# The last modulation block shared out anew between VectorE and TensorE, and the folded h fetched on GpSimd's queue

## The chip, the cores and the metric

The kernel runs on one core of a Trainium2 chip. A core has TensorE (matrix products; PE in the profile, PEld for its weight loads), VectorE (DVE), ScalarE (ACT), GpSimd (POOL) and SyncE (SP), which issues most of the DMAs. The metric is the device time of one launch, in microseconds (us); the time of before is the median of three runs.

## The reference

One layer of a diffusion backbone, in float32, for 128 context and 256 latent positions at width 2048. The part that the change touches is the adaptive modulation: for two condition vectors (context, latent), `silu(cond) @ w_ada + b_ada` gives six vectors of 2048 per condition, which shift, scale and gate the two sub-layers.

```python
mod = jax.nn.silu(cond) @ lw['w_ada'] + lw['b_ada']
sh1, sc1, ga1, sh2, sc2, ga2 = [m[:, None, :] for m in jnp.split(mod, N_MOD, axis=-1)]
h = rmsnorm(x, lw['norm_pre_mix']) * (1.0 + sc1) + sh1
m, s_f, s_b = mixer(h, s0_f, s0_b, n_chunks, lw)   # GLA and Fourier branches, gates, w_out
x = x + ga1 * rmsnorm(m, lw['norm_post_mix'])
h = rmsnorm(x, lw['norm_pre_ffn']) * (1.0 + sc2) + sh2
ff = (jax.nn.silu(h @ lw['w_ffn_gate']) * (h @ lw['w_ffn_up'])) @ lw['w_ffn_down']
x = x + ga2 * rmsnorm(ff, lw['norm_post_ffn'])
```

## The kernel before

Activations stand transposed (128 channels on the partitions, 384 positions along the free side). A weight half of 128x1024 comes by DMA (`raw`), ScalarE rounds it (`whi`, L256), VectorE takes the rest (`wlo`, L257), and TensorE makes three products per 128 columns (`A_hi,whi`, `A_lo,whi`, `A_hi,wlo`, L291). Weights are prepared some halves ahead, in four pairs of buffers. TensorE, ScalarE, VectorE and GpSimd each run their instructions in the order in which the program is written; nothing is reordered.

The stages follow each other: first norm and first modulation with the V projection; Q and K with the gated linear attention (GLA) beside the gate projections; gate units 22 and 23 with the folding of h for the Fourier branch; units 24 to 31 with the Fourier products; the merge; the output projection `w_out` (16 units of two halves of 24 products); a short stage that normalises and makes the input of the FFN; the FFN.

Side work is written as Python generators that are stepped once for each half (24 products):

- `ada_rest` (L656): modulation blocks (m, half) for m = 2, 3, 4. Each block takes 16 granules of `w_ada` (128x1024, tile `adaw`, two buffers); for a granule VectorE runs two operations, one for each condition, into `adacc` (L664 for the first granule, L666 for the others). Then eight small products sum over the partitions (L676), ScalarE copies (L640), two transposes (L644) and four small VectorE operations (L649 to L654) finish it. Five of the six blocks are made so.
- `ada_pe` (L684): the sixth block, (4, 1), is made by TensorE alone, four groups of four granules (tile `adax`), 16 products a group (L701), six steps apart, in the `w_out` stage. It ends in `ada_finish` (tile `evp`).
- `rate` (L715) says how many operations of `ada_rest` a step takes: in the GLA stage the number that the GLA generator yields, then 2.25 beside the Fourier products and 1.35 in `w_out`. After unit 12 of `w_out` both generators are run to their end.
- `folding` fetches the folded h (`hf_d`) in four pieces of 768 KB into two buffers (`fx`, L987 on SyncE's queue); `parts_of` (L1003) runs four products on each and splits it (L331, L332). The weights `wn` of these products are cleared by GpSimd (L994) and written by VectorE (L996). Ahead of that GpSimd clears `nyq` (L979), once the GLA stage's last ScalarE work on `qk` is done.

The stage ahead of the FFN (L1338 to L1470) sums squares (`wide_sum`), makes row factors `prow` (`rows2`, L1348), and fills two gaps with idle products on ones (`narrow_warm`, L1357). Then a loop over k makes h for channel tile k: VectorE `z` (L1412, L1418), ScalarE scale and shift with `mods` and rounding (`A_hi`, L1420, L1424), VectorE `A_lo` (L1436), VectorE and GpSimd the new x ahead of it (`t`, L1380; L1384), and TensorE the products of tile k-1 for three units of the FFN at once (L1454).

Of the kernel before, what the change touches and what calls it, by code (L numbers as in the profile page):

```python
# [11 lines left out]
F32 = mybir.dt.float32  # L12
# [9 lines left out]
P = 128  # L22
D = 2048
KT = D // P
TC = 128
TL = 256
T = TC + TL
# [10 lines left out]
G = 1024  # L38
# [69 lines left out]
def tile_step(ctx: ExitStack, tc: tile.TileContext, a, o):  # L108
    nc = tc.nc
    PE, ACT, DVE, POOL, SP = nc.tensor, nc.scalar, nc.vector, nc.gpsimd, nc.sync  # L110
# [80 lines left out]
    HEAD = 3  # L191
# [169 lines left out]
    hf_d = dram.tile([P, KT, T], F32, name="hf_d")  # L361
# [277 lines left out]
    def ada_finish(m, half, pr, ev):  # L639
        ACT.copy(ev, pr)  # L640
        yield True
        pt = pss.tile([P, 2, P], F32, tag="side", name="ptm")
        for b in range(2):
            PE.transpose(pt[:, b, :], ev[:, b * P : (b + 1) * P], ident)  # L644

        src = pt.rearrange("p b (j r) -> p j b r", r=32)
        mh = mods[:, m, 8 * half : 8 * half + 8, :]
        for c in range(2):
            DVE.tensor_copy(mh[:, :, c].rearrange("p (j b) -> p j b", b=2), src[:, :, :, c])  # L649
# [6 lines left out]
    def ada_rest(blocks):  # L656
        for m, half in blocks:
            acc = adap.tile([P, 2, 1024], F32, tag="adacc", name="adacc")
            for k in range(KT):
                w = adap.tile([P, 1024], F32, tag="adaw", name="adaw", bufs=2)  # L660
                SP.dma_start(w, a["w_ada"][m - 2, half, k])
                for c in range(2):
                    if k == 0:
                        DVE.tensor_scalar_mul(acc[:, c, :], w, cond[:, k, c : c + 1])  # L664
                    else:
                        DVE.scalar_tensor_tensor(  # L666
                            acc[:, c, :], w, cond[:, k, c : c + 1], acc[:, c, :], op0=ALU.mult, op1=ALU.add,
                        )
# [5 lines left out]
            for c in range(2):  # L674
                for j in range(4):
                    PE.matmul(  # L676
                        pr[32 * j : 32 * j + 32, :], selr[:, 32 * c : 32 * c + 32],
                        acc[:, c, j * 256 : (j + 1) * 256], start=c == 0, stop=c == 1,
                    )
            yield from ada_finish(m, half, pr, acc[:, 0, 0:256])  # L680

    def ada_pe(pool, cpad, ev, m, half, apart):

        def fetch(k0):  # L684

            ws = []
            for n, t in enumerate(("hid_hi", "hid_lo", "S0", "S1")):
                ws.append(pool.tile([P, G], F32, tag=t, name="adax", bufs=1))
                SP.dma_start(ws[n], a["w_ada"][m - 2, half, k0 + n])
            return ws  # L690

        pr = None
        for k0 in range(0, KT, 4):
            ws = fetch(k0)
            for _ in range(apart):
                yield
            if pr is None:
                pr = pss.tile([P, 256], F32, tag="side", name="pr")
            for n, w in enumerate(ws):
                for j in range(4):  # L700
                    PE.matmul(  # L701
                        pr[32 * j : 32 * j + 32, :], cpad[:, k0 + n, :], w[:, j * 256 : (j + 1) * 256],
                        start=k0 + n == 0, stop=k0 + n == KT - 1,
                    )
        yield from ada_finish(m, half, pr, ev)


    gates_d = dram.tile([32, P, T], F32, name="gates_d")
# [4 lines left out]
        return qk[:, h:8:4, t * P : (t + 1) * P]  # L713

    rate = [1.0]  # L715
    ada_gen = ada_rest([(m, half) for m in (2, 3, 4) for half in range(2)][:-1])
# [13 lines left out]
    with ExitStack() as s:  # L730
# [28 lines left out]
        def gla():  # L759
# [10 lines left out]
            for h in range(NH):  # L770
# [201 lines left out]
    with ExitStack() as s:  # L972
# [11 lines left out]
        fx = actp.tile([P, 2, 4, T], F32, tag="C_lo", name="fx")  # L984

        def fetch(b):
            SP.dma_start(fx[:, b % 2], hf_d[:, 4 * b : 4 * b + 4, :])  # L987

        fetch(0)
        fetch(1)  # L990
# [251 lines left out]
    with ExitStack() as s:  # L1242
# [16 lines left out]
        by_pe = ada_pe(pe, cpad, pd.tile([P, 256], F32, name="evp", bufs=1), 4, 1, 6)  # L1259

        qs = [pd.tile([P, T], F32, tag=f"qs{n}", name="qs", bufs=1) for n in range(3)]

# [78 lines left out]

        r = pd.tile([P, 2, 3], F32, name="r12", bufs=1)
        u = pd.tile([P, 2, 3], F32, name="u12", bufs=1)
        prow, prow2 = (pss.tile([P, T], F32, tag="side", name="prow") for _ in range(2))

        def rows2(dst, n):
            for t in range(3):
# [4 lines left out]
        hp = [psm.tile([P, T], F32, tag="mm", name="pmm") for _ in range(HEAD - 1)]  # L1352

        def narrow_warm(n):

            for _ in range(n):
                PE.matmul(hp[-2][:, 0:P], ones, ones, start=True, stop=True)  # L1357
# [81 lines left out]
        for k in range(KT + 1):  # L1439
            if k < KT:  # L1440
                res_b(k)
            if k:
                res_c(k - 1)

            for n in range(k + 2 + (k > 4), k + 3 + (k > 3)):
                if n < KT:
                    res_m(n)
                    res_a(n)
            if k:
                if k % 8 == 1:  # L1450
                    hw = [take() for _ in range(HEAD)]
                for j, m in ((0, 0), (1, 0), (0, 1)):
                    for u in range(HEAD):
                        PE.matmul(  # L1454
                            hp[u], hw[u][j][:, ((k - 1) % 8) * P : ((k - 1) % 8 + 1) * P], h2[m][:, k - 1, :],
                            start=k == 1 and j == m == 0, stop=k == KT and m == 1,
                        )
            if k in (9, 12):
                split(None, POOL)
                load()  # L1460
# [262 lines left out]
        n = 0  # L1723
# [500 lines left out]
```

## Time and profile before

| | us |
|---|---|
| median of three runs | 1922.1 (1920.74 to 1923.08) |
| the profiled execution | 1921.57 |
| its span | 1919.8 |
| granted TensorE clock in it | 0.998 of full speed |

The stages stand in the span (us) at 146 to 418 (Q, K, GLA), 418 to 437 (folding), 437 to 612 (Fourier products), 612 to 741 (merge), 741 to 877 (`w_out`), 877 to 911 (ahead of the FFN); the rest is the FFN. A row of the timeline gives the start, the duration, the engine, the line and operation, out<-in with shapes, how many, and in brackets the idle time of the engine just before and what ended it. A TensorE product of float32 operands counts as two records in the trace, so 16 products of L701 stand as x32. Products overlap in the pipeline: the distance from one start to the next is what a product costs, not its duration.

### The profile page before, as it was taken

Reading aid. Unit: us, or ns where it says so; the run is one execution under the profiler, and the core shown is the slowest. Engines: PE = TensorE matmul, PEld = TensorE weight load, DVE = VectorE, ACT = ScalarE, POOL = GpSimd, SP = SyncE. Lnnn points to the kernel's source line nnn. Section 1 sums busy time; section 2 is a strip of 40 time slices with the busy share of each in tenths; the row PEclk is TensorE's granted clock in tenths of the full one; section 3 lists DMA queues with packets and bytes.
Section 4 is the critical chain, followed back from the end, with each engine's and each line's share of the span. In section 5 each row is a group of like instructions: output and inputs, shape, how many; then the busy total and the mean of one; then the engine's idle time right before and its main releaser. Section 6 shows DMA issues by size and latency. Waiting matters only on the chain.

```text
span 1919.8 us, 28034 instructions
## 1 busy us (share of the span) xinstructions
PE 1898.7 (99%) x10396; PEld 1674.6 (87%) x10396; DVE 1634.2 (85%) x2104; ACT 1080.2 (56%) x1569; POOL 160.4 (8%) x189
## 2 busy tenths in 40 slices
PE   8999999999999999999999999999999999999997
PEld 5779999999999999999988888888888888888886
DVE  5677878787977897877799999999999999988985
ACT  4335545554447554446457666756666666666554
POOL 0000001000000000004000111111112021111001
PEclk9999999999999999999999999999999999999999
DMA  9986767777756787765449697988879797969563
GB/s 389 371 316 217 230 219 229 242 255 240 245 189 195 254 278 266 277 227 203 160 135 282 158 253 179 249 198 229 206 216 234 185 247 179 264 128 260 147 209 114
DMA packets 247529, 435.66 MB, mean 227 GB/s; under 512 B 45916, under 2 KB 150556, under 8 KB 242784
## 3 DMA queue, kind: packets, MB, share of 16 engines
q1 hardware_dynamic: 199792, 391.59, 61.1%
q0 software_dynamic: 18944, 33.63, 11.4%
q10 hardware_dynamic: 28656, 8.65, 2.5%
q8 instruction: 81, 1.33, 0.3%
q14 instruction: 56, 0.46, 0.1%
HBM read 369.05 MB, written 57.67 MB: 222 GB/s over the span
## 4 chain that ended last, share of the span: by engine, by line
PE 88%; DVE 4%; DMA 4%; ACT 2%; issue 1%; SPq 0%; DVEq 0%; ACTq 0%
PE pgu L1740 31%; PE pmm L291 26%; PE pdn L1740 10%; PE pds L1740 7%; PE pv L463 3%; PE pgm L446 1%; PE pfo L1103 1%; DVE wlo L257 1%; DMA slab<-in_w_ada 1%; PE px L481 1%; PE pmm L1454 1%; DMA raw<-in_w_gate 1%; ACT whi L256 1%; DMA raw<-in_w_out 1%; PE pfo L1104 1%
## 5 line engine op out<-in xcount | busy, mean ns | idle before, releaser
L291 PE MATMUL pmm<-A_hi,whi 128*128 128x384 f32 x1072 | 361.7, 337 | 0.0
L291 PE MATMUL pmm<-A_lo,whi 128*128 128x384 f32 x1072 | 358.6, 335 | 0.5 <-DVE A_lo L332 0.5
L291 PE MATMUL pmm<-A_hi,wlo 128*128 128x384 f32 x1072 | 358.7, 335 | 0.0
L1638 ACT CAST whi<-u 128x1024 fp32r<-128x1024 f32 x200 | 210.3, 1053 | 171.2 <-PE pds L1740 40.8
L1649 DVE TENSOR_TENSOR wlo<-u,whi 128x1024 fp32r<-128x1024 f32 x200 | 243.6, 1220 | 34.6 <-ACT whi L1638 32.5
L256 ACT CAST whi<-raw 128x1024 fp32r<-128x1024 f32 x163 | 170.7, 1051 | 158.5 <-DMA raw<-in_w_out 66.9
L1740 PE MATMUL pgu<-whi,A_hi 128*128 128x512 f32 x640 | 249.9, 391 | 0.0
L1740 PE MATMUL pgu<-whi,A_lo 128*128 128x512 f32 x640 | 249.1, 389 | 0.0
L257 DVE TENSOR_TENSOR wlo<-raw,whi 128x1024 fp32r<-128x1024 f32 x161 | 196.0, 1219 | 52.4 <-ACT whi L256 51.7
L1638 ACT CAST whi<-raw 128x1024 fp32r<-128x1024 f32 x157 | 164.9, 1052 | 91.3 <-PE pgu L1740 30.0
L291 PEld LDWEIGHTS pmm<-A_hi,whi 128*128 128x128 f32 x1072 | 201.2, 188 | 4.7 <-issue 3.3
L1649 DVE TENSOR_TENSOR wlo<-raw,whi 128x1024 fp32r<-128x1024 f32 x157 | 191.1, 1217 | 13.3 <-ACT whi L1638 11.3
L291 PEld LDWEIGHTS pmm<-A_lo,whi 128*128 128x128 f32 x1072 | 201.3, 188 | 1.0 <-DVE A_lo L332 0.8
L291 PEld LDWEIGHTS pmm<-A_hi,wlo 128*128 128x128 f32 x1072 | 201.2, 188 | 0.0
L666 DVE SCALAR_TENSOR_TENSOR adacc<-adaw,cond,adacc 128x1024 f32<-128x1024 f32 x150 | 187.6, 1278 | 12.9 <-DMA adaw<-in_w_ada 12.4
L1740 PE MATMUL pgu<-wlo,A_hi 128*128 128x512 f32 x640 | 185.7, 389 | 0.0
L1740 PEld LDWEIGHTS pgu<-whi,A_hi 128*128 128x128 f32 x640 | 120.1, 188 | 25.9 <-issue 0.8
L1740 PEld LDWEIGHTS pgu<-wlo,A_hi 128*128 128x128 f32 x640 | 120.2, 188 | 25.1
L1740 PEld LDWEIGHTS pgu<-whi,A_lo 128*128 128x128 f32 x640 | 120.2, 188 | 24.7
L1740 PE MATMUL pgu<-whi,S 128*128 128x512 f32 x400 | 116.6, 389 | 0.0
L1873 POOL DMA_DIRECT2D sums_d<-spare x64 | 58.3, 952 | 623.6 <-ACT spare L1869 602.3
L1740 PE MATMUL pdn<-whi,hid_hi 128*128 128x512 f32 x264 | 102.8, 389 | 0.0
(465 smaller groups left out, 3538.4 us busy)
## 6 DMA issues: line engine op xcount, KB each, us to landing
adaw<-in_w_ada SPq DMA_DIRECT2D x80, 512.0 KB, 4.4
raw<-in_w_d SPq DMA_DIRECT2D x70, 512.0 KB, 5.9
slab<-in_w_ada SPq DMA_DIRECT2D x32, 1024.0 KB, 9.5
raw<-in_w_gate SPq DMA_DIRECT2D x64, 512.0 KB, 4.6
raw<-in_w_g SPq DMA_DIRECT2D x48, 512.0 KB, 3.7
raw<-in_w_u SPq DMA_DIRECT2D x48, 512.0 KB, 5.1
u<-in_w_u SPq DMA_DIRECT2D x40, 512.0 KB, 6.0
u<-in_w_g SPq DMA_DIRECT2D x40, 512.0 KB, 9.3
```

The source lines that it names most:

```text
L256: ACT.copy(hi, raw)
L257: sub = lambda: eng.tensor_sub(lo, raw, hi.bitcast(F32))
L291: PE.matmul(dst, w[wi][:, k * n + n0 : k * n + n0 + P], x[xi][:, k0 + k, :], start=first and k == 0 and j == 0, stop=last and k == kts - 1 ...
L446: PE.matmul(pgv[q : q + 32, :], spad[:, k, :], slab[k // (KT // 2)][:, k % (KT // 2), :], start=k < 4, stop=k >= KT - 4,)
L463: PE.matmul(pv[2 * t + g], hT[x_][:, kb, t * P : (t + 1) * P], w_[:, g * 512 : (g + 1) * 512], start=kb == 0 and j == 0, stop=kb == KT - 1 ...
L481: PE.matmul(px, w_[:, u * P : (u + 1) * P], hT[x_][:, kb, :], start=j == 0, stop=j == 2)
L666: DVE.scalar_tensor_tensor(acc[:, c, :], w, cond[:, k, c : c + 1], acc[:, c, :], op0=ALU.mult, op1=ALU.add,)
L1103: PE.matmul(p, w[0][:, c], x[:, 0 : 2 * n], start=kh == k == 0, stop=False)
L1638: ACT.copy(hi, src)
L1649: DVE.tensor_sub(lo, src, hi.bitcast(F32))
L1740: PE.matmul(dst, stat[x_][m], mov(w[w_], m), start=first and w_ == m == x_ == 0, stop=last and w_ == m == 1, skip_group_check=any(more),)
L1873: POOL.dma_start(sums_d[k], u, accum_op=ALU.add)
```

## The change

Three things are changed.

1. The blocks. `ada_rest` takes the sixth block too, for its first 9 granules. `ada_pe` is left with one group of four granules (9 to 12), whose products go into the same accumulator as the partition sums of VectorE's part (`ada_products`, `ada_sums`), and are copied to `evp0`. The last three granules are loaded as halves into `ep0` to `ep5`, and their products (`late_products`) take the place of `narrow_warm(4)` and `narrow_warm(2)`; their sums stand in spare columns 384 to 511 of the PSUM banks of `prow` and of two of the three FFN accumulators. At k = 3 and k = 4 ScalarE copies these to `evp1` and `evp2`; at k = 6 six float32 products with the identity transpose the three parts and add them up, and `ada_finish`, now only four VectorE operations, writes `mods` for tiles 8 to 15. Granules of `adax` are fetched one a step instead of four at once.
2. The folded h is fetched by GpSimd's queue.
3. The GLA generator yields 3 or 4 where it yielded 2, for another of its steps less; `rate` becomes 2.5 beside the Fourier products and 1.75 in `w_out`.

```diff
+    def ada_sums(pr, acc, first, last):
+        for c in range(2):
+            for j in range(4):
+                PE.matmul(
+                    pr[32 * j : 32 * j + 32, :], selr[:, 32 * c : 32 * c + 32],
+                    acc[:, c, j * 256 : (j + 1) * 256], start=first and c == 0, stop=last and c == 1,
+                )
+    KV, KG = 9, 13
+    last_acc = []
...
-            for k in range(KT):
+            part = (m, half) == (4, 1)
+            for k in range(KV if part else KT):
...
+            if part:
+                last_acc.append(acc)
+                return
...
-        for k0 in range(0, KT, 4):
-            ws = fetch(k0)
-            for _ in range(apart):
-                yield
...
+        for n in range(KT - KG):
+            late.append(ep[2 * n : 2 * n + 2])
+            for j in range(2):
+                SP.dma_start(late[n][j], src[KG + n, :, 512 * j : 512 * j + 512])
+            yield
+        while not last_acc:
+            yield
+        yield
+        pr = pss.tile([P, 256], F32, tag="side", name="pr")
+        for n, w in enumerate(group):
+            ada_products(pr, cpad, KV + n, w, n == 0, False)
+        ada_sums(pr, last_acc[0], False, True)
+        ACT.copy(evs[0], pr)
...
-                yield 2
+                yield 3 + h % 2
                 if h == 0:
-                    yield 2
                     yield 2
...
-            SP.dma_start(fx[:, b % 2], hf_d[:, 4 * b : 4 * b + 4, :])
+            POOL.dma_start(fx[:, b % 2], hf_d[:, 4 * b : 4 * b + 4, :])
...
-        rate[0] = 2.25
+        rate[0] = 2.5
...
-        rate[0] = 1.35
+        rate[0] = 1.75
...
-        narrow_warm(4)
+        late_products(prm[0], (0, 1))
...
-        narrow_warm(2)
+        late_products(prm[1], (2,))
...
+            if k in (3, 4):
+                for b in range(2):
+                    ACT.copy(evs[k - 2][:, b * P : (b + 1) * P], prm[k - 3][b])
+            if k == 6:
+                for b in range(2):
+                    for n, ev in enumerate(evs):
+                        PE.matmul(prm[0][b], ev[:, b * P : (b + 1) * P], ident, start=n == 0, stop=n == 2)
+                ada_finish(4, 1, prm[0])
```

**VectorE at the end of unit 12 of `w_out`.** `qs` and `pr` (L1276 to L1280, now L1309 to L1313) are the statistics of the unit that TensorE has just ended. In before the next work behind them finishes the fifth and the sixth block:

```order
L1276 TENSOR_TENSOR qs<-qs,sq 128x384
L1278 TENSOR_TENSOR pr<-Blo,Clo 128x384
L1279 TENSOR_TENSOR qs<-qs,pr 128x384
L1280 TENSOR_TENSOR qs<-qs,sq 128x384
L649 COPY mods<-ptm 128x8 x2
L651 TENSOR_TENSOR mods<-mods,bsc_82 128x16
```

Of the change the same place, from the statistics of unit 11 to those of unit 12 and what is behind them:

```order
L1313 TENSOR_TENSOR qs<-qs,sq 128x384
L686 SCALAR_TENSOR_TENSOR adacc<-adaw,cond,adacc 128x1024
L257 TENSOR_TENSOR wlo<-raw,whi 128x1024
L686 SCALAR_TENSOR_TENSOR adacc<-adaw,cond,adacc 128x1024 x2
L257 TENSOR_TENSOR wlo<-raw,whi 128x1024
L1309 TENSOR_TENSOR qs<-qs,sq 128x384
L1311 TENSOR_TENSOR pr<-Blo,Clo 128x384
L1312 TENSOR_TENSOR qs<-qs,pr 128x384
L1313 TENSOR_TENSOR qs<-qs,sq 128x384
L686 SCALAR_TENSOR_TENSOR adacc<-adaw,cond,adacc 128x1024
L257 TENSOR_TENSOR wlo<-raw_8691,whi 128x1024
```

The last operation of the sixth block stands behind unit 12's statistics. On TensorE the end of unit 12 was, in before, the four transposes of both blocks:

```order
L291 MATMUL pmm<-A_lo,whi 128x384
L291 MATMUL pmm<-A_hi,wlo 128x384
L644 MATMUL ptm<-ident,adacc 128x128 x2
L644 MATMUL ptm<-ident,evp 128x128 x2
L291 MATMUL pmm<-A_hi,whi 128x384
```

and is now the one group and, behind it, the sums that read `adacc`:

```order
L291 MATMUL pmm<-A_lo,whi 128x384
L291 MATMUL pmm<-A_hi,wlo 128x384
L667 MATMUL pr<-adax,cpad 32x256 x16
L659 MATMUL pr<-adacc,selr 32x256 x8
L291 MATMUL pmm<-A_hi,whi 128x384
```

**The stage ahead of the FFN, k = 6.** TensorE of the change, between the products of tiles 5 and 6 (L1502 was L1454):

```order
L1502 MATMUL pmm<-A_lo,whi 128x384 x3
L1512 MATMUL prow<-ident,evp_7620 128x128
L1512 MATMUL prow<-ident,evp_7621 128x128
L1512 MATMUL prow<-ident,evp_7622 128x128
L1512 MATMUL prow<-ident,evp_7620 128x128
L1512 MATMUL prow<-ident,evp_7621 128x128
L1512 MATMUL prow<-ident,evp_7622 128x128
L1502 MATMUL pmm<-A_hi,whi 128x384 x3
```

and VectorE of the change at that place:

```order
L1484 TENSOR_TENSOR A_lo<-z,A_hi 128x384
L1428 TENSOR_TENSOR t_9104<-Blo,prow 128x384
L710 COPY mods<-prow 128x4x2 x2
L712 TENSOR_TENSOR mods<-mods,bsc_82 128x16
L715 TENSOR_TENSOR mods<-mods,norms 128x16
L1466 TENSOR_TENSOR z<-Chi,prow 128x384
```

The six products and the four small operations are new there; `z` of tile 7 now stands behind operations that read what the six products write.

**GpSimd at the folding.** Before, the last rows ahead of the stage's own and those of the stage:

```order
L757 DMA wnr<-in_w_in 128x8x1 x4
L979 MEMSET nyq 128x256
L994 MEMSET wn_4345 128x512
L1123 MEMSET wr 128x1024 x2
L1257 MEMSET cpad 128x512
```

and of the change:

```order
L790 DMA wnr<-in_w_in 128x8x1 x4
L1011 MEMSET nyq 128x256
L1019 DMA fx<-hf_d 128x1536 x2
L1026 MEMSET wn_4357 128x512
L1019 DMA fx<-hf_d 128x1536 x2
L1155 MEMSET wr 128x1024 x2
```

The first two fetches now stand behind the clearing of `nyq`, and that of `wn` behind them.

More of the change, by code (lines that the diff above doesn't have):

```diff
@@ L673, in ada_rest @@
             pr = pss.tile([P, 256], F32, tag="side", name="pr")
[L674 to L692, printed above, removed]
-        for k0 in range(0, KT, 4):
-            ws = fetch(k0)
-            for _ in range(apart):
-                yield
[L697 to L705, printed above, removed]
@@ new lines, in ada_rest, with ada_finish @@
+            ada_sums(pr, acc, True, True)
+            ev = acc[:, 0, 0:256]
+            ACT.copy(ev, pr)
+            yield True
+            pt = pss.tile([P, 2, P], F32, tag="side", name="ptm")
+            for b in range(2):
+                PE.transpose(pt[:, b, :], ev[:, b * P : (b + 1) * P], ident)
+            ada_finish(m, half, [pt[:, b, :] for b in range(2)])
+    def ada_finish(m, half, pt):
+        mh = mods[:, m, 8 * half : 8 * half + 8, :]
+        for b in range(2):
+            DVE.tensor_copy(mh[:, b:8:2, :], pt[b].rearrange("p (j r) -> p j r", r=32)[:, :, 0:2])
+        bc = lambda v: v[:, 8 * half : 8 * half + 8].unsqueeze(2).to_broadcast([P, 8, 2])
+        DVE.tensor_add(mh, mh, bc(bsc1[:, 1, :] if m == 4 else cols[:, m, :]))
+        w1 = {2: 1, 4: 2, 5: 3}.get(m)
+        if w1 is not None:
+            DVE.tensor_mul(mh, mh, bc(norms[:, w1, :]))
@@ new lines, in ada_pe @@
+    def ada_pe(pool, ep, cpad, evs):
+        src = a["w_ada"][2, 1]
+        group, late = [], []
+        for n, t in enumerate(("hid_hi", "hid_lo", "S0", "S1")):
+            w = pool.tile([P, G], F32, tag=t, name="adax", bufs=1)
+            group.append([w[:, 0 : G // 2], w[:, G // 2 : G]])
+            SP.dma_start(w, src[KV + n])
+            yield
[6 more added lines that the diff above has]
+            yield
+        yield
+        pr = pss.tile([P, 256], F32, tag="side", name="pr")
[3 more added lines that the diff above has]
+        ACT.copy(evs[0], pr)
+        last_acc.append(late)
@@ L715, in tile_step @@
     rate = [1.0]
-    ada_gen = ada_rest([(m, half) for m in (2, 3, 4) for half in range(2)][:-1])
+    ada_gen = ada_rest()
     ada = meted(ada_gen, rate)
@@ L1258, in tile_step @@
         ACT.copy(cpad[:, :, 0:2], cond)
-        by_pe = ada_pe(pe, cpad, pd.tile([P, 256], F32, name="evp", bufs=1), 4, 1, 6)
+        evs = [pd.tile([P, 256], F32, name=f"evp{n}", bufs=1) for n in range(3)]
+        by_pe = ada_pe(pe, ep, cpad, evs)
         qs = [pd.tile([P, T], F32, tag=f"qs{n}", name="qs", bufs=1) for n in range(3)]
@@ L1343, in tile_step, with late_products @@
         u = pd.tile([P, 2, 3], F32, name="u12", bufs=1)
-        prow, prow2 = (pss.tile([P, T], F32, tag="side", name="prow") for _ in range(2))
+        prows = [pss.tile([P, 512], F32, tag="side", name="prow") for _ in range(2)]
+        prow, prow2 = (x[:, 0:T] for x in prows)
+        prm = [[x[:, T:512] for x in prows]]
+        late_ada = last_acc[1]
+        def late_products(dst, ns):
+            for n in ns:
+                for b in range(2):
+                    for j in range(4):
+                        PE.matmul(
+                            dst[b][32 * j : 32 * j + 32, :], cpad[:, KG + n, :],
+                            late_ada[n][j // 2][:, 256 * (j % 2) + P * b : 256 * (j % 2) + P * b + P],
+                            start=n == ns[0], stop=n == ns[-1],
+                        )
         def rows2(dst, n):
@@ L1350, in rows2 @@
                 )
-        hp = [psm.tile([P, T], F32, tag="mm", name="pmm") for _ in range(HEAD - 1)]
+        hps = [psm.tile([P, 512], F32, tag="mm", name="pmm") for _ in range(HEAD - 1)]
+        hp = [x[:, 0:T] for x in hps]
+        prm.append([x[:, T:512] for x in hps])
         def narrow_warm(n):
@@ L1457, in tile_step @@
                         )
+            if k in (3, 4):
+                for b in range(2):
+                    ACT.copy(evs[k - 2][:, b * P : (b + 1) * P], prm[k - 3][b])
+            if k == 6:
+                for b in range(2):
+                    for n, ev in enumerate(evs):
+                        PE.matmul(prm[0][b], ev[:, b * P : (b + 1) * P], ident, start=n == 0, stop=n == 2)
+                ada_finish(4, 1, prm[0])
             if k in (9, 12):
```

10 lines of the change are left out of this document (8 added, 2 removed).

## The prediction

> **What bounds the kernel now.** I read the busy shares and the chain of work first, then the chain of waits in order of time, then the timeline at each place that the change touches.
>
> ```profile
> PE 1898.7 (99%) x10396; PEld 1674.6 (87%) x10396; DVE 1634.2 (85%) x2104; ACT 1080.2 (56%) x1569; POOL 160.4 (8%) x189
> PE 88%; DVE 4%; DMA 4%; ACT 2%; issue 1%; SPq 0%; DVEq 0%; ACTq 0%
> ```
>
> TensorE is busy 99% of the span. So a product taken away saves its time, as long as no wait takes its place; VectorE has room, but not much, and it runs in order.
>
> ```profile
> 418.00:437.00 19.00, 16.11 (x110) 13.77 (x109) 14.42 (x15) 9.22 (x12) 0.78 (x2) 1.00 0.87 299
> 437.00:612.00 175.00, 175.00 (x1093) 172.06 (x1093) 140.97 (x167) 84.21 (x134) 1.92 (x2) 1.00 0.67 215
> 741.00:877.00 136.00, 135.47 (x875) 130.07 (x875) 105.87 (x131) 61.17 (x101) 0.53 (x1) 1.00 0.71 249
> ```
>
> These are the windows by stage (length, then busy time of PE, PEld, DVE, ACT, POOL, then granted clock, DMA share, GB/s). Beside the Fourier products and in `w_out` TensorE never rests; the folding stage is the one place here where it loses time, 2.89 us of 19.
>
> **The change part by part.** First the groups taken out of `w_out`. The chain of waits has stretches of L291 with holes between them:
>
> ```profile
> 741.85 21.45 PE pmm L291 x122
> 765.17 25.18 PE pmm L291 x144
> 792.21 25.18 PE pmm L291 x144
> ...
> 893.38 17.46 PE pmm L1454 x99
> ```
>
> 741.85 + 21.45 = 763.30, and L291 resumes at 765.17: a group of 16 products costs 1.87 us (the next hole, 790.35 to 792.21, 1.86). Each unit of `w_out` lasts 25.18 / 3 = 8.39 us. What stands at the end of the block in before:
>
> ```profile
> 844.37 1.07 PE L676 MATMUL pr<-adacc,selr 128*32 128x256 f32 x16
> 845.26 1.91 PE L701 MATMUL pr<-adax,cpad 128*32 128x256 f32 x32
> ...
> 851.37 0.38 PE L644 MATMUL ptm<-ident,adacc 128*128 128x128 f32 x2
> ...
> 851.73 0.42 PE L291 MATMUL pmm<-A_hi,whi 128*128 128x384 f32 x1
> ```
>
> Eight partition sums cost 845.26 - 844.37 = 0.89, four transposes 0.36. TensorE loses three groups (3 x 1.87 = 5.61) and two transposes (0.18), and gains eight sums (0.89): 5.61 + 0.18 - 0.89 = **4.90 us less work**.
>
> But the new sums add a wait. They stand at the very end of unit 12, because both generators are run out there, and their second half reads an operation that VectorE has behind unit 12's own statistics. The same place in before shows how late that is (TensorE's last product of the unit is followed by 851.37):
>
> ```profile
> 851.57 0.49 ACT L1265 ACTIVATE sq<-pmm 128x384 f32<-128x384 f32 x1 [2.34 <-PE pmm L291]
> ...
> 852.09 0.56 DVE L1276 TENSOR_TENSOR qs<-qs,sq 128x384 f32<-128x384 f32 x1 [1.61 <-ACT sq L1265]
> ...
> 854.26 0.23 DVE L649 COPY mods<-ptm 128x8 f32<-128x8 f32 x2
> ...
> 839.36 1.28 DVE L666 SCALAR_TENSOR_TENSOR adacc<-adaw,cond,adacc 128x1024 f32<-128x1024 f32 x1
> ```
>
> After the statistics VectorE is free at 854.26, 2.89 us behind the unit's end; the operation takes 1.28, so the sums may go on 4.17 to 4.2 us after it. TensorE is there after one group and half the sums, 1.87 + 0.45 = 2.32. It **waits 1.9 us**, with all of `w_out` queued behind it in TensorE's order. VectorE must also not be late:
>
> ```profile
> 766.73 2.47 DVE L666 SCALAR_TENSOR_TENSOR adacc<-adaw,cond,adacc 128x1024 f32<-128x1024 f32 x2
> ...
> 774.59 1.28 DVE L666 SCALAR_TENSOR_TENSOR adacc<-adaw,cond,adacc 128x1024 f32<-128x1024 f32 x1
> ```
>
> From 766.73 to 774.59 stands one unit's work with three such operations: 7.86 us. By the changed order the units ahead of unit 12 have three or four; four need 7.86 + 1.2 = 9.06, 0.67 over the unit's 8.39, and the three of the next give 0.53 back. The last unit has three, so at most some tenths of lag are left. The wait is from 1.9 (no lag) to about 4 (a transfer of weights that holds up ScalarE's copies in front). I take 2.2, near the row that shows the place. Sum for `w_out`: -4.90 + 2.2 = **-2.7 us**.
>
> Then the late products, in place of idle ones:
>
> ```profile
> 878.24 1.11 PE L1357 MATMUL pmm<-ones 128*128 128x128 f32 x8
> ...
> 878.71 0.56 DVE L1365 TENSOR_TENSOR qs<-qs,pr 128x384 f32<-128x384 f32 x1
> ...
> 879.42 1.52 PE L1338 MATMUL pst<-ones,qs 128*128 128x64 f32 x12
> ...
> 1137.44 0.64 PE L1693 MATMUL pr<-acc,selr 128*32 128x128 f32 x16
> ...
> 1138.15 0.27 ACT L1698 COPY acc<-pr 128x128 f32<-128x128 f32 x1 [2.59 <-PE pr L1693]
> ```
>
> Eight products of the late shape (x16) take 0.64 in another stage; sixteen take at most 1.28. The gap from 878.24 to 879.42 is 1.18, since what follows waits for the addition that ends at 879.27. The second gap gets eight for four idle ones (0.64 for 0.61). Cost: **+0.1 us**, from 0 to the price in a rival below.
>
> Then the loop ahead of the FFN, k = 6:
>
> ```profile
> 880.77 0.89 PE L1348 MATMUL prow<-ident,r 128*128 128x128 f32 x6
> 881.50 0.61 PE L1357 MATMUL pmm<-ones 128*128 128x128 f32 x4
> ...
> 894.29 0.56 DVE L1418 TENSOR_TENSOR z<-Chi,prow 128x384 f32<-128x384 f32 x1
> ...
> 854.82 0.23 DVE L649 COPY mods<-ptm 128x8 f32<-128x8 f32 x2
> ...
> 895.04 0.68 PE L1454 MATMUL pmm<-A_hi,whi 128*128 128x384 f32 x3
> ...
> 908.05 0.48 ACT L1424 CAST A_hi<-z 128x384 fp32r<-128x384 f32 x1
> ...
> 909.12 0.68 PE L1454 MATMUL pmm<-A_hi,whi 128*128 128x384 f32 x3
> ```
>
> Three float32 products of 128x128 fill 880.77 to 881.50, 0.243 each; six cost 1.46. They come behind tile 5's products, which end at 895.04. VectorE's copies wait for them (895.04 + 1.46 + 0.1 = 896.6), the four small operations take 854.82 - 854.26 = 0.56, and only then `z` of tile 7 may start: about 897.2 instead of 894.29. ScalarE's four copies at k = 3 and 4, 0.27 each by the row at 1138.15, delay tile 5's products by up to 0.5 more, since ScalarE makes `A_hi` in the same order and TensorE's next products into the same banks wait for the copies too. So the chain through `z`, `A_hi`, `A_lo` moves by 2.9 to 3.4 us (897.2 - 894.29, and 0.5). TensorE has little lead over it: tile 15's `A_hi` ends at 908.05 + 0.48 = 908.53, its products start at 909.12, 0.59 later. From 893.38 on the chain of waits shows TensorE without a hole, so whatever is beyond that lead is lost. A shift of 3.4 less 0.59 is 2.8; with a smaller ScalarE part and no lead used, 2.9. I take **+2.9 us**; the ends are 1.46 (only the products count) and 4.
>
> Then the folding. TensorE loses time twice:
>
> ```profile
> 411.73 1.71 ACT L933 ACTIVATE qk<-qk,rs 128x256 f32<-128x256 f32 x4
> ...
> 418.07 0.31 POOL L979 MEMSET nyq<- 128x256 f32 x1 [87.27 <-ACT qk L933]
> ...
> 419.79 0.26 DVE L996 TENSOR_TENSOR wn<-wnr 128x64 f32<-128x64 f32 x1
> ...
> 420.15 0.54 PE L1003 MATMUL bnp<-fx,wn 128*32 128x194 f32 x8 [1.33 <-issue]
> ...
> 436.31 0.54 PE L1003 MATMUL bnp<-fx,wn 128*32 128x194 f32 x8 [1.55 <-DMA fx<-hf_d]
> ```
>
> The chain of waits has the last fetch, the views by tile the issues (durations in ns), and the windows the stretch in which the first two pieces now fall:
>
> ```profile
> 430.25 6.02 DMA fx<-hf_d
> ...
> L987 SPq DMA_DIRECT2D fx<-hf_d x4: 319/354/423, 364.3 to 430.2; - x4
> L757 POOL DMA_DIRECT2D wnr<-in_w_in x16: 880/880/1077, 151.2 to 329.9; - x16
> ...
> 413.00:418.00 5.00, 5.00 (x31) 5.00 (x30) 5.00 (x5) 3.56 (x8) 0.00 (x0) 1.00 0.74 244
> ```
>
> At 420.15 it waited for `wn` on VectorE (419.79), at 436.31 for the last fetch (6.02 us on the wire). With the GLA one step sooner, GpSimd's `nyq` comes near 411.73 + 1.71 = 413.4 instead of 418.07; two issues of 0.88 follow (the `wnr` row), so the first piece is issued at about 413.9 and lands, at 6.0 us, at 420.0 or a little later beside the second piece. Before, those two were issued from 364.3 on, far ahead. One wait goes, another of like length takes its place: **0 us**, from -2.9 (both holes of the stage closed) to +5.2, the two pieces' 1.57 MB at the stage's own 299 GB/s, if nothing hides them.
>
> [...]
>
> Last, of VectorE's 18 new operations about ten run ahead of `w_out`: some four of them beside the Fourier products (5 us in a stage where VectorE has 175.00 - 140.97 = 34 us free), some six in the GLA. TensorE was busy 175.00 of 175.00 us there. **+0.3 us**, from 0 to 1.28 for one operation that lands in front of a weight TensorE waits for.
>
> Sum: -2.7 + 0.1 + 2.9 + 0 + 0.3 = +0.6. The profiled execution took 1921.57 us, which gives 1922.2; from the median, 1922.1, it gives 1922.7. I say **1922.4**.
>
> **The rivals.** *B: the waits are smaller than I make them.* VectorE's last operation finds a hole ahead of the statistics (no 2.2), the k = 6 step costs only its 1.46, and the folding loses its first hole (the 1.33 of the row at 420.15): -4.90 + 0.1 + 1.46 - 1.33 + 0.3 = -4.4, or 1922.1 - 4.4 = 1917.7 by the median. For it: VectorE is not full in any stage. Against it: both orders are fixed, and the rows above show the delays. *C, slower: the folded h lands late.* The first piece is issued 50 us later than before, into a stretch that moves 244 to 299 GB/s already. TensorE asks for it about 418.8 (420.15 - 1.33), and stood until 420.15 anyhow; each us of landing after 420.15 is a us lost. Past 423.6 (9.7 us after the issue) the sum passes the bound for slower; a landing at 424.4 costs 4.3 and gives 1926.7. For it: ScalarE and TensorE work in order, so a late piece holds up the weights behind it. Against it: six us sufficed at 430.25. *D: the change doesn't do what it says*: the late products do not fit their gaps. At the 256-wide price, 1.87 / 16 = 0.117 each, 24 cost 2.8 for gaps of 1.18 and 0.61: 1922.4 + 1.0 = 1923.4.
>
> **How the numbers follow.** Forecast 0.54 (own range 1919.5 to 1925), B 0.18, C 0.18, D 0.10. A measurement can tell some 0.2% (3.8 us) from no change: faster is below 1918.3, slower above 1925.9. Faster: nearly all of B, 0.17. Slower: most of C and the upper edge of the forecast and D, 0.19. Same: 0.64. The range that leaves out half of B and half of C: 1917.6 to 1926.4.
>
> **What would show it.** In the changed profile: one group in `w_out` with a wait of about 2 us on `adacc` behind it (none: B); six products of L1512 near 892 followed by a hole of about 1.4 us on TensorE and VectorE's copies ended by PE; `bnp` still ended by `fx` or `wn`, with the holes of the folding stage near 3 us in all (none: B; over 6: C); the gap ahead of the second `wide_sum` unchanged (longer: D). I am wrong if the loop at k = 6 catches up, or if VectorE's greater load delays weights in a stage where TensorE was never waiting.

## The result, and the profile after

The change takes **1938.2 us** in the median (1936.3 to 1942.4), the kernel before, run beside it, 1922.2 (1920.7 to 1927.1): the ratio is 1.0085, with a 95% interval from 1.0074 to 1.0096. That is slower by 16 us, where 1922.4 was forecast and the range ended at 1926.4. The profiled execution of the change took 1942.4 us (span 1940.4), the longest of its six, 20.6 us over the span of before; the stages below account for 20.4 of these. Its mean granted clock is 0.993, where four of the six executions have 0.996: the profile holds more time at a low clock than most, and its stages add up to more than the median's 16.

The busy times and the chain of work, in the same two lines as before:

```profile
PE 1906.0 (98%) x10362; PEld 1680.7 (87%) x10362; DVE 1654.0 (85%) x2122; ACT 1079.8 (56%) x1573; POOL 162.2 (8%) x193
PE 79%; DVE 9%; DMA 6%; issue 2%; ACT 2%; SPq 0%; DVEq 0%; POOL 0%; ACTq 0%
```

TensorE has 34 instructions fewer and yet is busy 7.3 us more: the same products took longer. In the chain its share fell from 88% to 79%; VectorE's rose from 4% to 9%, the DMAs' from 4% to 6%. What TensorE waited for, by the list of waits (us in total, times, the longest):

```profile
PE pr L659 <- DVE adacc L686: 4.9, 2, 2.9
PE bnp L1035 <- issue: 4.3, 1, 4.3
...
PE pmm L291 <- DVE A_lo L332: 2.8, 2, 1.9
...
PE pf L1210 <- DVE wlo L257: 1.5, 1, 1.5
PE px L1090 <- DVE fs L1140: 1.2, 2, 0.8
PE ptm L703 <- ACT adacc L699: 1.0, 1, 1.0
```

In before the same list has 0.5 for `A_lo`, 1.3 and 1.6 for `bnp`, and nothing for the sums. Only one of the two waits on `adacc` was in the prediction. The windows by stage (columns as in the prediction; the last five are short ones at four of the holes):

```profile
423.00:437.00 14.00, 9.74 (x53) 8.29 (x52) 6.88 (x9) 5.11 (x7) 0.53 (x1) 0.76 1.02 394
437.00:612.00 175.00, 173.75 (x1094) 168.36 (x1093) 139.31 (x162) 79.36 (x127) 2.44 (x3) 1.00 0.65 214
741.00:877.00 136.00, 130.09 (x766) 125.81 (x765) 114.83 (x136) 57.85 (x94) 0.53 (x1) 0.97 0.71 243
245.00:249.00 4.00, 1.94 (x21) 0.89 (x20) 4.00 (x8) 0.36 (x1) 0.00 (x0) 1.00 0.51 144
249.00:252.00 3.00, 3.00 (x12) 3.00 (x11) 3.00 (x8) 1.67 (x4) 0.00 (x0) 0.51 0.81 300
428.40:433.00 4.60, 4.60 (x20) 4.00 (x21) 3.02 (x3) 1.81 (x3) 0.53 (x1) 0.50 1.01 412
757.00:760.00 3.00, 2.71 (x9) 2.71 (x10) 1.05 (x2) 2.17 (x4) 0.53 (x1) 0.60 0.67 220
867.00:871.00 4.00, 4.00 (x18) 3.98 (x15) 0.00 (x0) 0.58 (x2) 0.00 (x0) 0.59 0.67 232
```

The seventh number (the granted clock) is the one that the prediction never asked for: behind each long hole it falls to about a half for some 3 to 5 us. To place the loss I set the start of each product of TensorE against that of the same product in before; the difference is its delay. It grows like this:

| stage | delay at its end, us | gained in it | forecast |
|---|---|---|---|
| GLA, to 413 | 5.3 | +5.3 | part of +0.3 |
| folding, to 437 | 9.7 | +4.4 | 0 |
| Fourier products and merge, to 750 | 12.6 | +2.9 | part of +0.3 |
| start of `w_out`, to 762 | 17.0 | +4.4 | none |
| the rest of `w_out` | 16.8 | -7.3 to 857, then +7.1 at unit 12 | -2.7 |
| ahead of the FFN | 20.4 | +3.6 | +3.0 |

**The GLA.** From 146 to 418, before and then the change:

```profile
146.00:418.00 272.00, 272.00 (x1770) 268.76 (x1769) 223.13 (x289) 143.92 (x252) 17.53 (x25) 1.00 0.72 228
```

```profile
146.00:418.00 272.00, 268.98 (x1740) 264.95 (x1739) 225.34 (x291) 141.13 (x249) 17.10 (x25) 0.99 0.70 223
```

The timeline of the change, at the sums of the first block (start, duration, engine, line):

```profile
242.57 1.29 DVE L686 SCALAR_TENSOR_TENSOR adacc<-adaw,cond,adacc 128x1024 f32<-128x1024 f32 x1 [2.38 <-DMA adaw<-in_w_ada]
...
245.16 0.64 PE L659 MATMUL pr<-adacc,selr 128*32 128x256 f32 x8
...
246.52 1.28 DVE L686 SCALAR_TENSOR_TENSOR adacc<-adaw,cond,adacc 128x1024 f32<-128x1024 f32 x1
...
247.85 0.64 PE L659 MATMUL pr<-adacc,selr 128*32 128x256 f32 x8 [2.06 <-DVE adacc L686]
```

With three and four operations a step, VectorE outran its two `adaw` buffers and waited 2.38 us for a granule; its last operation then stood behind the GLA's own work (`qi`, `ki`, `ko`, `kc`) at 246.52, and the sums, which TensorE now reaches early, waited 2.06 for it. A wait of 1.0 for `ptm`, near 352, and the clock behind the first hole make up most of the rest of the stage's 5.3. In the chain of waits of the change, 24 products ahead of such a hole and behind it, for three holes:

```profile
155.74 4.16 PE pmm L291 x24
...
248.49 5.97 PE pmm L291 x24
...
429.25 6.27 PE pmm L291 x24
435.98 4.39 PE pmm L291 x24
...
867.09 26.66 PE pmm L291 x144
```

5.97 against 4.16: the half clock costs 1.8 us more. Behind the folding's hole it is 6.27 against the 4.39 of the next 24, 1.9 us. The last row stands behind unit 12 of `w_out`: 144 products in 26.66, against 24.98 at the same place in before, 1.7 us:

```profile
851.97 24.98 PE pmm L291 x144
```

**The folding.** GpSimd and TensorE in the timeline, and the fetches in the view by tile (the last line gives the time from issue to landing):

```profile
418.76 0.31 POOL L1011 MEMSET nyq<- 128x256 f32 x1 [87.93 <-ACT qk L965]
...
419.26 1.09 POOL L1019 DMA_DIRECT2D fx<-hf_d  x2 [0.18 <-issue]
```

```profile
L1019 POOL DMA_DIRECT2D fx<-hf_d x4: 528/537/558, 419.3 to 439.3; - x4
...
DMA to landing us min/median/max: 4.4/7.7/11.0
```

`nyq` came at 418.76: the 413.4 of the prediction and the 5.3 us of the GLA's delay. That shift moves TensorE's demand just as much. But the first piece landed at about 428.1, 8.8 us behind its issue where 6.0 had been reckoned. The two pieces issued together landed after 8.8 and 11.0 us, the next two, issued one at a time, after 6.7 and 4.4, on the same queue. The DMA engines were full meanwhile (share 1.02 in the window from 423 to 437, against 0.87 from 418 to 437 in before). So two pieces at once, beside the weights, are the likely reason; no run fetched the first piece alone. TensorE stood from 423.8 to 428.2, and went on at clock 0.50 until 433.

**`w_out`, unit 12**, and **the head**, in the timeline:

```profile
862.92 0.61 PE L659 MATMUL pr<-adacc,selr 128*32 128x256 f32 x8
...
865.07 1.28 DVE L686 SCALAR_TENSOR_TENSOR adacc<-adaw,cond,adacc 128x1024 f32<-128x1024 f32 x1
...
866.40 0.70 PE L659 MATMUL pr<-adacc,selr 128*32 128x256 f32 x8 [2.86 <-DVE adacc L686]
...
906.96 0.56 DVE L1466 TENSOR_TENSOR z<-Chi,prow 128x384 f32<-128x384 f32 x1 [0.92 <-ACT evp L1508]
...
912.68 1.50 PE L1512 MATMUL prow<-ident,evp 128*128 128x128 f32 x12
...
913.55 0.17 DVE L710 COPY mods<-prow 128x8 f32<-128x8 f32 x1 [1.56 <-PE prow L1512]
...
915.31 1.00 ACT L1468 ACTIVATE z<-z,mods 128x128 f32<-128x128 f32 x2 [2.96 <-DVE z L1466]
...
915.79 0.80 PE L1502 MATMUL pmm<-A_lo,whi 128*128 128x384 f32 x3 [0.56 <-DVE A_lo L1484]
```

Both mechanisms are as predicted: the sums wait 2.86 for VectorE's last operation, which stands behind the statistics, and the six products (1.50) hold up VectorE's copies and so the chain `z`, `A_hi`, `A_lo`.

### The profile page after: what moved, and what is told of

It is laid out like the page before. It is cut to its first block, busy times and chain, and to the rows that moved or that the text cites. A ratio compares the mean times of both kernels' runs of the same rounds, so it can differ in the third digit from the quotient of the medians.

```text
span 1940.4 us, 28005 instructions
## 1 busy us (share of the span) xinstructions
PE 1906.0 (98%) x10362; PEld 1680.7 (87%) x10362; DVE 1654.0 (85%) x2122; ACT 1079.8 (56%) x1573; POOL 162.2 (8%) x193
## 4 chain that ended last, share of the span: by engine, by line
PE 79%; DVE 9%; DMA 6%; issue 2%; ACT 2%; SPq 0%; DVEq 0%; POOL 0%; ACTq 0%
PE pgu L1796 31%; PE pmm L291 19%; PE pdn L1796 10%; PE pds L1796 7%; PE pv L463 3%; DVE wlo L257 3%; DVE adacc L686 2%; DMA raw<-in_w_out 2%; DMA adaw<-in_w_ada 2%; PE pgm L446 1%; DMA slab<-in_w_ada 1%; PE px L481 1%; ACT whi L256 1%; PE pmm L1502 1%; PE pfo L1135 1%
## 5 line engine op out<-in xcount | busy, mean ns | idle before, releaser
L686 DVE SCALAR_TENSOR_TENSOR adacc<-adaw,cond,adacc 128x1024 f32<-128x1024 f32 x166 | 207.0, 1279 | 19.0 <-DMA adaw<-in_w_ada 18.7
L1705 DVE TENSOR_TENSOR wlo<-raw,whi 128x1024 fp32r<-128x1024 f32 x157 | 191.2, 1218 | 10.9 <-ACT whi L1694 10.5
```

Of the source, the lines that this page charges most:

```text
L686: DVE.scalar_tensor_tensor(acc[:, c, :], w, cond[:, k, c : c + 1], acc[:, c, :], op0=ALU.mult, op1=ALU.add,)
L1705: DVE.tensor_sub(lo, src, hi.bitcast(F32))
```

## The experiments

Theory: the loss lies in four waits (the first block's sums, the folded h, the sums at unit 12, the finish at k = 6), and in the half clock behind the long holes. Rival: it is VectorE's load of 18 more operations, or the changed traffic as a whole, wherever it stands. Kernels that start from before are named so; the others start from the change. Before ran beside all of them, at 1921.4 to 1922.4 us in the median.

**Two parts alone, added to before.** First the GLA's pace:

```diff
-                yield 2
+                yield 3 + h % 2
                 if h == 0:
-                    yield 2
                     yield 2
```

> The kernel before with the change's GLA pacing alone (yields of 3 and 4 for 2, one yield less; VectorE does the same 160 operations, earlier). Theory G (the quicker pacing makes VectorE wait for its granules and late for the first block's sums, and a hole of over 2 us costs TensorE half its clock for some 3.4 us after it): a hole of about 2.4 us near 245, a granted clock near 0.6 behind it, +4 to +6 us at the end of the GLA stage, 1926 to 1928 in all; the folding stage then differs little from before. Rival (pacing alone is harmless, the delay at 245 comes from something else in the change): no such hole, 1920 to 1923.

Measured: 1925.5 us (1923.9 to 1929.2), ratio 1.0026, from 1.0015 to 1.0036, a little under what the theory expected. The wait is there, the low clock behind it is not:

```profile
247.81 0.64 PE L676 MATMUL pr<-adacc,selr 128*32 128x256 f32 x8 [2.24 <-DVE adacc L666]
```

```profile
248.20:251.20 3.00, 3.00 (x24) 2.82 (x17) 3.00 (x7) 2.03 (x4) 0.00 (x0) 1.00 0.77 236
```

24 products in these 3 us where the change had 12, at clock 1.00. So the pace alone costs some 4 us, and whether a hole of 2.2 us halves the clock is not decided by its length alone (the last section has the two holes side by side). Then the queue of the folded h:

```diff
-            SP.dma_start(fx[:, b % 2], hf_d[:, 4 * b : 4 * b + 4, :])
+            POOL.dma_start(fx[:, b % 2], hf_d[:, 4 * b : 4 * b + 4, :])
```

> The kernel before with the folded h fetched on GpSimd's queue alone. Theory P (the first fetch now waits behind nyq, which waits for the GLA's last ScalarE work at about 418, and lands 8 to 9 us later, near 427; TensorE wants it near 419): a hole of 6 to 8 us ahead of the first bnp, clock at half behind it (+1.8), +8 to +10 us: 1930 to 1932. Rival (the fetches on that queue land quickly, and the change's hole there came from the GLA stage's delay): +0 to +3 us.

Measured: 1928.7 us (1927.6 to 1929.9), ratio 1.0038, from 1.0024 to 1.0051: less than the theory's 1930 to 1932, though its hole and its half clock are there. Waits of TensorE, and the windows of the folding stage and of the time behind its hole:

```profile
PE bnp L1003 <- issue: 7.3, 1, 7.3
```

```profile
418.00:437.00 19.00, 11.70 (x63) 10.25 (x62) 8.55 (x10) 6.84 (x10) 1.76 (x5) 0.73 0.90 328
425.60:431.00 5.40, 5.10 (x21) 4.52 (x22) 4.16 (x4) 2.62 (x3) 0.53 (x1) 0.50 0.98 376
```

One word of code costs some 7 us: the fetch is issued at 417.6, since GpSimd must clear `nyq` first, and TensorE stands for 7.3 us.

**The same two parts taken out of the change.** SyncE's queue again for `fx`:

> The changed kernel with the folded h fetched on SyncE's queue again. Theory P: the hole of 4.3 us ahead of the first bnp and the half clock behind it go, -4 to -5.5 us against the change: 1932.5 to 1934. Rival (the hole is due to the later or fuller traffic, whatever the queue): within 1.5 us of the change's 1938.

Measured: 1933.7 us (1932.8 to 1934.2), 4.5 less than the change. And the old pace in the GLA again:

> The changed kernel with the GLA pacing of before; the six operations that VectorE then does later end up behind unit 12's statistics. Theory G+S: the holes of the GLA stage go (-4 to -5.5 us by the end of that stage, with the half clock), the sums at unit 12 wait some 6 x 1.25 = 7 us longer than in the change: +1 to +4 us in all, 1939 to 1942. Rival (pacing moves nothing but VectorE's spare time): the GLA gain stays, 1933 to 1934.

Measured: 1939.2 us (1938.6 to 1940.1), 1.1 more than the change, whose times (1936.3 to 1942.4) include these. The holes of the GLA are gone, but the operations that it did not take are run out at unit 12, and `fx` comes as late as in the kernel with the queue alone:

```profile
PE pr L659 <- DVE adacc L686: 9.0, 1, 9.0
PE bnp L1036 <- issue: 7.8, 1, 7.8
```

So the parts of the change lean on each other: the pace is needed for the nine granules, and the pace makes the queue a little less harmful. That is why undoing the pace alone gains nothing, though it costs 4 us by itself.

**The half clock.** Products on ones ahead of the four long waits, so that TensorE is busy while it waits; they write where the next products start anew:

```diff
+    def idle(dst, n):
+        for _ in range(n):
+            PE.matmul(dst[:, 0:P], ones, ones, start=True, stop=True)
...
+            if (m, half) == (2, 0):
+                idle(pr, 9)
...
+        idle(pr, 11)
...
+        idle(bnp, 17)
...
+                if i == 0 and g == 0:
+                    idle(p, 9)
```

> The changed kernel with idle products on ones put ahead of the four places where TensorE has holes of over 2 us (9 ahead of the first block's sums, 17 ahead of the first bnp, 9 ahead of w_out's first unit, 11 ahead of the group at unit 12; some 0.24 us each). The holes become busy time and the waits stay. Theory H (each such hole costs 1 to 2 us more by the half clock behind it): granted clock back to 0.998, -4 to -7 us against the change: 1931 to 1934. Rival (the low clock is not made by the holes): clock stays near 0.995 and the time within 1.5 us of the change or longer.

Measured: 1934.1 us (1933.4 to 1936.0), 4.1 less than the change. The windows behind the first block's sums and behind the late `fx`:

```profile
248.20:251.20 3.00, 3.00 (x18) 3.00 (x19) 3.00 (x8) 1.50 (x4) 0.00 (x0) 1.00 0.80 295
...
426.00:431.00 5.00, 5.00 (x40) 4.34 (x39) 3.11 (x3) 1.88 (x3) 0.53 (x1) 1.00 1.03 413
```

Clock 1.00 in both, where the change had 0.51 and 0.50, and the idle products stand where the waits were. So of the 16 us about 4 are the clock, lost behind the waits and not in them. (In this execution, the longest of its four, the mean granted clock is 0.997 where the other three have 0.999, and TensorE still waits for `fx` twice, 3.4 us in all, the longer 2.6.)

**`w_out`.** The change with `rate` 2.0 for 1.75, which ends VectorE's last operation ahead of unit 12's statistics:

> The changed kernel with 2.0 operations a step in w_out for 1.75: VectorE's last operation of the block stands a unit and a half earlier. Theory S (the sums at unit 12 wait 2.9 us for an operation behind the unit's own statistics, plus the half clock): the hole of 2.9 us goes, -3 to -5 us, 1933 to 1935. Rival (VectorE is full in w_out, so more of its work per unit only makes it late elsewhere): a hole of a like length at another place in w_out, within 1.5 us of the change.

Measured: 1934.5 us (1934.0 to 1936.6), 3.7 less; TensorE's wait on the sums of unit 12 is gone. And the change with 16 of VectorE's 18 operations of the sixth block left out (granules 1 to 8, and their transfers):

> The change with VectorE doing one granule of block (4,1) where it did nine: 16 of its operations and their transfers are left out of w_out (and of the result), everything else as in the change. Theory (in w_out the change pays for the order of VectorE: the sums of unit 12 wait for its last operation, with half clock behind): the hole of 3.2 us and the half clock behind it go, about 5 us, 1932 to 1934; the losses of the GLA (5), the folding (4), the start of w_out (4) and the head (3.6) stay. Rival (VectorE's whole load, its transfers among it, slows all of w_out): 8 us or more go, under 1931.

Measured: 1934.8 us (1932.7 to 1937.6), 3.3 less than the change, a little above what the theory expected and far from the rival's 8. Leaving the operations out gains no more than ending them earlier: in the change, with its 1.75 operations a step, it is their place and not their load that costs.

**The head.** The operands of the six products are ready long before k = 6. Here the products go into the bank `zx` at k = 2, VectorE's four operations follow at k = 4, and ScalarE's copies to `evp1` and `evp2` stand ahead of the loop:

```diff
-            if k in (3, 4):
-                for b in range(2):
-                    ACT.copy(evs[k - 2][:, b * P : (b + 1) * P], prm[k - 3][b])
-            if k == 6:
+            if k == 2:
...
+            if k == 4:
+                ada_finish(4, 1, [zx[:, b * P : (b + 1) * P] for b in range(2)])
```

> The changed kernel with the finish of the last block moved in the stage ahead of the FFN: evp1 and evp2 are copied before the loop, the six transposing products go to idle columns of the zx bank at k = 2, and VectorE's four operations stand at k = 4, when the products have long ended. Theory K (the step at k = 6 costs 3.6 us since VectorE stands still until the six products end, of which TensorE's own work is 1.46): -1.7 to -3 us against the change, 1935 to 1936.5, no hole behind the six products. Rival (the head's loss is the work itself, or late products and copies): within 0.7 us of the change.

Measured: 1936.5 us (1934.1 to 1937.8), 1.7 less. The times overlap with those of the change, but the traces are clear: the delay gained in the head falls from 3.6 to 1.6, about the 1.46 of the products alone, and it is 1.6 again in the two kernels below that finish the block early, and 3.6 in the runs above that start from the change and leave the finish at k = 6.

**All mended.** The old pace, SyncE's queue, the early finish, `rate` 2.5 beside the Fourier products and 2.1 in `w_out`; the nine granules, the one group and the late products stay:

> The changed kernel with all of it mended: GLA pacing of before, folded h on SyncE's queue, 2.1 operations a step in w_out (so that no operation stands behind unit 12's statistics), and the finish at k = 2 and 4. If the losses are those four and no others: 20 us less 5 (GLA), 5 (folding), 4 (sums), 2 (finish), and 4 for half clocks: 1917 to 1921, at or below before (1921.4), since TensorE has 4.9 us less work in w_out and 1.5 to 2 more ahead of the FFN. Rival (VectorE's 18 operations cost in any place): 1923 to 1928, with new holes in w_out or beside the Fourier products.

Measured: 1923.4 us (1920.1 to 1925.3), ratio 1.0005, from 0.9996 to 1.0014. The four repairs bring back 14.8 of the 16 us, and what is left is level with before. But the theory, that the losses are those four and no others, had 1917 to 1921; the measured time lies above that, at the lower end of the rival's 1923 to 1928, and the new holes in `w_out` that the rival named are there. Five of the ten times lie from 1920.1 to 1922.4 and five from 1924.4 to 1925.3; the profile is of one of the longer:

```profile
PE pmm L291 <- DVE wlo L257: 3.5, 4, 1.6
...
PE bnp L1036 <- issue: 2.3, 1, 2.3
```

```profile
741.00:877.00 136.00, 130.76 (x786) 126.17 (x785) 122.09 (x142) 61.11 (x100) 0.53 (x1) 1.00 0.72 242
```

VectorE is busy 122.09 us of 136 there (105.87 in before), and TensorE waits four times for `wlo`: at 2.1 operations a step VectorE's load does cost, and nine granules are too many. So the last kernel gives VectorE five, TensorE two groups of four in `w_out`, and runs 1.7 operations a step:

```diff
-    KV, KG = 9, 13
+    KV, KG = 5, 13
...
+        group = yield from fetch(KV + 4)
+        for _ in range(2):
+            yield
+        for n, w in enumerate(group):
+            ada_products(pr, cpad, KV + 4 + n, w, False, False)
...
-        rate[0] = 2.1
+        rate[0] = 1.7
```

> As the run with all parts mended (first pace in the GLA, SyncE's queue for the folded h, the finish of block (4,1) early), but VectorE takes 5 granules of block (4,1) where it took 9, TensorE two groups of four (granules 5 to 12) and the last three as late products; 1.7 operations a step in w_out, which ends VectorE's last one ahead of unit 12's statistics. Theory (what is left of the loss there is VectorE too full in w_out: holes of 0.7 to 1.8 us on wlo, about 5 us): against the mended run one group more costs 1.9 us, the holes on wlo go (-3 to -5): end 1 to 3 us ahead of it, 1920 to 1922.5, level with before or up to 0.1% faster. Rival (the holes on wlo come from ScalarE or the transfers and not from VectorE's share): one group more and nothing saved, about 1925.

Measured: 1920.4 us (1918.4 to 1921.9), before beside it 1922.4: ratio 0.9987, from 0.9978 to 0.9995, as the theory expected. It is some 2 us faster than before: less than the 0.2% named in the prediction, but the interval does not reach 1. Its `w_out` has TensorE busy all the time again, with VectorE at 114.46:

```profile
741.00:877.00 136.00, 135.99 (x878) 131.33 (x876) 114.46 (x138) 61.89 (x104) 0.00 (x0) 1.00 0.73 251
```

## Why the prediction was wrong, by its steps

- **VectorE's load in the GLA and the Fourier stage, +0.3** (0 to 1.28): this step failed most. It priced some six more operations in the GLA at next to nothing because TensorE "was busy 175.00 of 175.00"; that is the row of the Fourier products, and the GLA's own (272.00 of 272.00) would only have said that TensorE did not wait there in before. What the change alters there is the pace: VectorE runs out of granules, and TensorE comes to a block's sums before VectorE's last operation, the same kind of wait that the prediction worked out for unit 12. The stage gained 5.3 us of delay, 1.8 of it by the clock; the pace alone costs about 4.
- **The folding, 0:** rival C held in its mechanism; that its price (4.3, for a landing 10.5 us behind the issue) is near the 4.4 measured is luck. By C's own rule the landing 8.8 us behind the issue costs 2.6, and the half clock, which C lacked, adds 1.9. The step that failed is "lands, at 6.0 us": the row stood for one piece in a stage with DMA share 0.87, and was used for two at once in a full one. The kernel with the queue alone stood for 7.3 us in the same place and ended 7.3 us later, beyond the range's +5.2. The landings of 4.4 to 11.0 us decide, where 6.0 was reckoned; the issues, reckoned at 0.88 us, took 0.53 each.
- **`w_out`, -2.7:** the work went about as reckoned (-7.3 us by 857, where four groups of nearly 2.0 each are gone; the one that is left follows at unit 12), and the wait was 2.86 for a forecast 2.2; VectorE came to unit 12's statistics from a `wlo` that it had begun at 861.93, which the place in before did not show. What the sum put at nothing are 1.7 us of half clock behind that wait, and 4.4 at the start of the stage: `A_lo` came late by up to 1.94 there, then clock 0.60. In the lists of waits `A_lo` stands at 2.7 or 2.8 us in the runs with the new pace and the new queue, 1.3 with idle products ahead of it, at 1.6 and 1.7 with the new pace on SyncE's queue, and at 0.9 at most wherever the old pace stands, in before too (0.5). It is long only where the new pace and the new queue come together. In the trace VectorE's work for `A_lo` stands behind a granule's operation and a `wlo` (751.57 to 754.06). No run took this wait away by itself, so its cause stays open.
- **The late products, +0.1:** the two groups of `wide_sum` around the first gap start 2.65 us apart in before and 2.64 in the change, so these products fit; rival D, that they do not, was not seen.
- **k = 6, +2.9:** right, mis-sized by 0.7. VectorE's `z` also waited 0.92 us for ScalarE's copies of `evp1` (the row at 906.96); only ScalarE's time had been counted. Both read one bank of `prow`; no run shows whether that is the reason.
- **B** (smaller waits) did not come. Of the remaining +2.9 between 437 and 750, the waits on `fs` beside the Fourier products (1.2) and on `wlo` in the merge (1.5, with clock 0.50 behind it from 679.1 to 682.5) are most, and part of the latter is made good before `w_out`; no run settles whether they follow from the traffic or from VectorE.

The prediction summed each stage as if the others stood still, and it counted a hole as its length. Its range ended at +4.3 because it left out half of rival C and had no term for the pace or for the clock.

## What to carry to other kernels

Before a transfer is moved to another queue, find out what stands ahead of it in that queue's engine, and price its landing at the traffic of the new place. A faster pace of side work on one engine is also an earlier demand by the engine that consumes it: look for the last operation ahead of each hand-over, at every block and not only at the one that was edited. Count what stands behind a TensorE hole too: in the change, holes of 2.06, 2.86 and 4.3 us cost 1.7 to 1.9 us more behind them, where the clock was 0.50; one of 2.24 us with the pace alone did not, as the next section shows.

## What the runs showed of the hardware

Behind holes of 2.06 us (the first block's sums), 2.86 (unit 12), 4.3 (`fx`) and 7.3 us (the queue alone) TensorE went on at clock 0.50. Behind 2.24 us with the pace alone it stayed at 1.00, and with products on ones in the hole it stayed at 1.00 too. In the trace of the change, up to its last 30 us, the stretches at 0.50 start at 249.04, 426.53, 679.12, 757.63 and 866.85; each lasts 3.41 us, the one at `fx` 6.83, and from the first start to the others it is 52, 126, 149 and 181 times 3.413 us. With the queue alone the low clock lasted some 10.2 us by its windows (0.69 over the 7.2 us from 418.40, 0.50 to 431, 0.92 to 433). Here is the first block's sums in steps of 3.41 us, in the change and with the pace alone, whose edges are an estimate, counted back in such steps from its own half clock at 1918.66 (length, busy time of PE, granted clock, DMA share, GB/s):

```profile
245.63:249.04 3.41, 1.35 (x15) 1.00 0.59 168
249.04:252.45 3.41, 3.41 (x13) 0.50 0.76 284
```

```profile
242.72:246.13 3.41, 2.85 (x22) 1.00 0.32 105
246.13:249.54 3.41, 1.73 (x14) 1.00 0.58 187
249.54:252.95 3.41, 3.41 (x25) 1.00 0.90 282
```

The change's hole lies in one step, which leaves 2.06 us of it without a product; the hole with the pace alone lies, by that estimate, across an edge, 0.56 and 1.68 us on either side. From 140 to 1900 us of the change's trace, five such steps at full clock have 2.06, 2.42, 1.48, 2.29 and 2.86 us without a product; they end at the five starts above, so each is followed by 0.50, and no other step at full clock has over 0.96. In before's trace, in steps counted back from its one stretch at 0.50 (from 1911.10 on), one step has 1.55 (433.12 to 436.53) and is followed by 1.00. So a hole of 2 us or a little more cost those 1.8 us in one place and nothing in another, and where it lay on these steps is, by the estimate, the difference. No run moved one hole alone across an edge, and no trace shows what sets the steps.
